# Four heads' base-block products of the recurrence in one run and one PSUM bank, where they stood in two runs and four banks

## The chip, the cores and the metric

The kernel runs on one core of a Trainium2 chip. The metric is the device time of one execution in microseconds (us). The kernel before took 920.47 us, the median of 3 runs (920.27 to 921.49).

## What is computed

Two decoder layers over 512 tokens of width 1024 in fp32. Each layer normalises x, multiplies it with one wide input weight, sends the columns through two branches, multiplies the joined result with an output weight, normalises and adds x. One branch is sliding-window attention; the other, which the change touches, is a gated linear recurrence with 8 heads of a 128x128 state:

```python
def hybrid_layer(x, w_in, w_out, g_pre, g_post, lb, g_head, sinks):
    h = rms_norm(x, g_pre)
    proj = jnp.einsum('bsd,de->bse', h, w_in)
    q_h, f_h, i_h, z_h, q_a, k_a, v_a, z_a = jnp.split(proj, SPLIT_POINTS, axis=-1)
    o_h = hgrn2(q_h, f_h, i_h, lb)
    o_h = rms_norm(o_h, g_head).reshape(B, S, HG_WIDTH).astype(z_h.dtype) * jax.nn.silu(z_h)
    ...
    y = jnp.einsum('bse,ed->bsd', jnp.concatenate([o_h, o_a], axis=-1), w_out)
    return x + rms_norm(y, g_post)

def hgrn2(q, f_logit, i, lb):
    # S_t = diag(f_t) S_{t-1} + (1 - f_t) i_t^T,  o_t = S_t^T q_t
    ...
    def step(state, xs):
        qch, kch, vch, b = xs
        ...
        scores = jnp.einsum('bhtd,bhsd,bhtsd->bhts', qch, kch, decay)
        o = jnp.einsum('bhts,bhsv->bhtv', scores, vch)
        o = o + jnp.einsum('bhtd,bhdv->bhtv', qch * jnp.exp(b), state)
        ...
```

## The kernel before, in words

**Projections.** All weight matrices are split in two fp32r halves (high and low), and each product of a 128-row weight piece takes three matmuls of 128x128 by 128x512 into a PSUM bank of the pool `pj` (3 banks); these are the matmuls of line 293, 3,084 for the two layers' large weights and 192 more for k and v. ScalarE makes the high half of a piece (L181), VectorE or GpSimd the low half (L182). One *step* (`step()`, L276) issues three such matmuls. A table of due times orders the conversions at least 20 steps ahead of the step that needs them.

**The merge.** Everything else runs in between. `merge` (L50) takes several generators, each with a total weight, and always advances the one with the smallest share done; a generator says with each `yield` how much weight it has spent. One of the streams is "the steps up to the end of a slab of weights", 1.0 each. So the weights decide after how many projection steps the next part of the recurrence is issued. In each layer the calls are at L980 to L983: the attention is merged with the steps up to the second slab of f and q columns, `prepare(0)` with the next slab, then `prepare(2)`, `hgrn(0)` and `prepare(4)` in a chain, then `prepare(6)` and `hgrn(4)`. `HG_N` is the total weight that `hgrn` yields. Matmuls issued through `pin` keep their place in the program; other engines' instructions are ordered by a scheduler.

**The recurrence.** The causal 128x128 score matrix of each head and each of four 128-token blocks is built by levels. `prepare(a)` handles heads a and a+1: it makes the scaled copies `qb` and `kb` (L712 to L717) in a pair of temporary tiles, and zeroes the matrix `As` (both heads in one tile of 128x1024, L704). The base products, `spread` (L689), give the 2x2 blocks on the diagonal: 16 matmuls per head, each with a 32-column stationary piece and 32 moving columns, placed on one of four column groups of the array by `tile_position`. In fp32 each is two matmuls in the profile, so a head is 32 matmuls there and two heads are a run of 64. `keep_spread` (L697) copies the valid entries under a mask into `As` with VectorE. Heads a and a+1 with a = 0 or 4 have their spread at the end of `prepare` (L724), into two banks of the pool `sc`; heads a+2 and a+3 have it at the start of `hgrn` (L733), into the two banks of `ac`.

Then `hgrn` does six levels (hh = 2, 4, ... 64). Levels 2 to 16 are a run of 128 matmuls of 32 columns by 16 (L750) for the four heads; level 32 has 64 (L756) and level 64 has 32 (L761). After each level's run, VectorE multiplies q (L768), GpSimd multiplies k (L769), and VectorE (L778) or ScalarE (L783, L788) copies the level's products into `As`. Then come transposes, states and outputs (L796 to L831).

Temporary tiles come from rotating pools: tag `b` has 2 buffers of 128x1024, `s` has 3 of 128x512, `u` has 1 and `a` has 2 of 128x1024.

Of the kernel before, what the change touches and what calls it, by code (L numbers as in the profile page):

```python
# [20 lines left out]
NT = SEQ // 128  # L21
# [11 lines left out]

W_BUFS = 9
RAW_BUFS = 4
HG_N = 53.5
VLAG = 4
QWAIT = 8
ROT_WAIT = 8
# [10 lines left out]
def merge(*streams):  # L50
    live = [[g, 0.0, float(total)] for g, total in streams]
    while live:
        s = min(live, key=lambda e: e[1] / e[2])
        try:
            s[1] += next(s[0]) or 1.0
        except StopIteration:
            live.remove(s)


def chain(*gens):  # L60
    for g in gens:
        yield from g
# [8 lines left out]
def hybrid_kernel(ctx: ExitStack, tc: tile.TileContext, x, wkv, win, wout, g_pre, g_post, lbp, ghead, sinks,  # L71
                  gcol_c, cos_f, sin_f, cos_t, sin_t, masks_c, out):
    nc = tc.nc
    P = 128
# [9 lines left out]
    def pin(ins):  # L84
        return tc.keep_in_program_order(ins)
# [8 lines left out]
    def sc():  # L94
        sc_turn[0] += 1
        return sc_tiles[sc_turn[0] % SC]

    def ac():
        ac_turn[0] += 1
        return ac_tiles[ac_turn[0] % len(ac_tiles)]  # L100

    def tmp(tag, dt=F32, n=1):

        t = tp.tile([P, n, 512] if n > 1 else [P, 512], dt, tag=tag, name=tag, bufs=TB[tag])
        return t
# [25 lines left out]
    for l in range(1, DEPTH):  # L131
        i = plan_order.index((l, "kv"))
# [224 lines left out]
    def halves(tag):  # L357
        t = tmp(tag, n=2)
        return [t[:, 0], t[:, 1]]
# [8 lines left out]
    class Norm:  # L368
# [47 lines left out]
        def rest(self, c):  # L416
            self.turn(c)
            self.high(c)
            self.low(c)
            if self.tt == NT - 1 and c == 1:  # L420
                state["limit"] = None
# [21 lines left out]
    def layer(l, last):  # L443
# [240 lines left out]

        on = {}

        As, kbs, qbs, tots, quad = {}, {}, {}, {}, {}

        def spread(j, bank):  # L689

            for n in range(NT):
                for b in range(4):
                    c = slice(n * P + 32 * b, n * P + 32 * b + 32)
                    pin(nc.tensor.matmul(bank[32 * b:32 * b + 32, c], lhsT=kbs[j][:, c], rhs=qbs[j][:, c], start=True, stop=True,
                                         tile_position=(0, 32 * b)))

        def keep_spread(j, bank):  # L697
            nc.vector.copy_predicated(As[j].rearrange("p (n t) -> p n t", n=NT), bmask.unsqueeze(1).broadcast_to([P, NT, P]),
                                      bank.rearrange("p (n t) -> p n t", n=NT))

        def prepare(a):

            t = tmp("a", n=2)
            nc.gpsimd.memset(t, 0.0)  # L704
            blocks = lambda t, w: t.rearrange("p (b j) -> p b j", j=w)
            for j in range(a, a + 2):
                As[j] = t[:, j - a]
                f, k, q = quad[j] = fT.pop(j), kT.pop(j), qT.pop(j)
                f2, k2, q2 = (blocks(t, 2) for t in (f, k, q))
                qb, kb = halves("b")  # L710
                qb2, kb2 = blocks(qb, 2), blocks(kb, 2)
                nc.vector.reciprocal(kb2[:, :, 1], f2[:, :, 1])  # L712
                nc.scalar.copy(qb2[:, :, 0], q2[:, :, 0])
                nc.vector.tensor_tensor(qb2[:, :, 1], q2[:, :, 1], f2[:, :, 1], op=ALU.mult)
                nc.scalar.copy(kb2[:, :, 0], k2[:, :, 0])
                nc.vector.tensor_tensor(kb2[:, :, 1], kb2[:, :, 1], k2[:, :, 1], op=ALU.mult)
                qbs[j], kbs[j] = qb, kb  # L717

                nc.gpsimd.tensor_tensor(k2[:, :, 0], k2[:, :, 0], f2[:, :, 1], op=ALU.mult)
                nc.vector.tensor_tensor(q2, qb2, f2[:, :, 0].unsqueeze(2).broadcast_to([P, SEQ // 2, 2]), op=ALU.mult)  # L720
                nc.vector.tensor_tensor(f2[:, :, 0], f2[:, :, 0], f2[:, :, 1], op=ALU.mult)
                tots[j] = f2[:, :, 0]
                yield 3.5
            if a % 4 == 0:  # L724
                banks = [sc(), sc()]
                for i in range(2):
                    spread(a + i, banks[i])
                for i in range(2):
                    keep_spread(a + i, banks[i])

        def hgrn(a):
            hs = [(j, *quad.pop(a + j)) for j in range(4)]
            banks = [ac(), ac()]  # L733
            for i in range(2):
                spread(a + 2 + i, banks[i])
            for i in range(2):
                keep_spread(a + 2 + i, banks[i])
            yield 1.5
            for hh in (2, 4, 8, 16, 32, 64):
                nb = SEQ // (2 * hh)  # L740
                per, qu = nb // NT, nb // NT // 4
# [1 line left out]
                for j, f, k, q in hs:  # L743
                    L, i = Ls[j // 2], j % 2
                    qv = q.rearrange("p (b two j) -> p b two j", two=2, j=hh)
                    if hh <= 16:
                        for n in range(NT):
                            for b in range(4):
                                o_, blk, c = n * P + 32 * b, n * per + b * qu, 256 * i + n * 64 + 16 * b
                                pin(nc.tensor.matmul(L[32 * b:32 * b + 32, c:c + 16], lhsT=k[:, o_:o_ + 32],  # L750
                                                     rhs=qv[:, blk:blk + qu, 1, :], start=True, stop=True, tile_position=(0, 32 * b)))
                    elif hh == 32:
                        for n in range(NT):
                            for b in range(2):
                                o_, r_, c = n * P + 64 * b, 64 * b + 32 * (n % 2), 64 * i + n // 2 * 32
                                pin(nc.tensor.matmul(L[r_:r_ + 32, c:c + 32], lhsT=k[:, o_:o_ + 32],  # L756
                                                     rhs=q[:, o_ + 32:o_ + 64], start=True, stop=True, tile_position=(0, r_)))
                    else:
                        for n in range(NT):
                            o_, b, c = n * P, n % 2, 128 * i + n // 2 * 64  # L760
                            pin(nc.tensor.matmul(L[64 * b:64 * b + 64, c:c + 64], lhsT=k[:, o_:o_ + 64],  # L761
                                                 rhs=q[:, o_ + 64:o_ + 128], start=True, stop=True))
                for two in (hs[:2], hs[2:]):
# [9 lines left out]
                    for j, f, k, q in two:  # L773
                        A, L, i = As[a + j], Ls[j // 2], j % 2
# [200 lines left out]
        def run():  # L975
            rest = lambda key: (through(key), remaining(key))
            until(lambda: 1 in qs)
            for _ in range(QWAIT):
                step()
            merge((att_stream([(g, n) for g in range(4) for n in range(NT)]), 4 * NT + VLAG + SLOW[0] * (SLOW[1] - 1)), rest(("in", l, FQ)))  # L980
            merge((prepare(0), 7.0), rest(("in", l, FQ + 1)))
            merge((chain(prepare(2), hgrn(0), prepare(4)), HG_N + 14), rest(("in", l, FQ + 3)))
            merge((chain(prepare(6), hgrn(4)), HG_N + 7), rest(("out", l, "h0")))  # L983
            kv_room.add(l + 1)
            drain(through(("out", l, "h1")))
# [47 lines left out]
    m, n = head[0], head[1]  # L1033
# [43 lines left out]
    amask, bmask = masks[:, 0:128], masks[:, 128:256]  # L1077
# [40 lines left out]
    for run in [layer(l, l == DEPTH - 1) for l in range(DEPTH)]:  # L1118
        run()
# [60 lines left out]
```

## Time and profile before

| | us | share of the span |
|---|---|---|
| profiled execution, its own time | 920.82 | |
| its span, first to last instruction | 919.1 | |
| TensorE matmuls (PE) busy | 903.7 | 98% |
| weight loads (PEld) busy | 751.6 | 82% |
| VectorE (DVE) busy | 668.2 | 73% |
| ScalarE (ACT) busy | 464.2 | 51% |
| GpSimd (POOL) busy | 273.7 | 30% |
| VectorE copies of `keep_spread` (L698), 16 | 10.9 | 1.2% |

The granted TensorE clock was 0.999 of full speed over the span. Rows of the timeline give start and duration of an instruction or of a merged series of equal ones; matmuls overlap their successors, so the distance between two starts says what a matmul costs, not its duration.

### The profile page before, as it was taken

The numbers are of one execution on the slowest core, as the hardware profiler recorded it, in microseconds if no ns is written. First come the engines' busy times: TensorE is split into PE (matmuls) and PEld (weight loads), VectorE is DVE, ScalarE is ACT, GpSimd is POOL, SyncE is SP. The second block draws the span as 40 slices with busy tenths as digits, with TensorE's granted clock in tenths as the row PEclk, the third lists the DMA queues.
The fourth block names the chain that finished last, engine by engine and source line by source line (L and its number), as shares of the span: only waits on it lengthen the run. The fifth ranks groups of instructions, "written<-read, shape, count | busy, mean of one in ns | idle before, by whom it ended". The sixth has DMA issues, their size and how long they took to land.

```text
span 919.1 us, 19004 instructions
## 1 busy us (share of the span) xinstructions
PE 903.7 (98%) x7240; PEld 751.6 (82%) x7240; DVE 668.2 (73%) x1326; ACT 464.2 (51%) x1100; POOL 273.7 (30%) x292
## 2 busy tenths in 40 slices
PE   8999999999999999999999999999999999999997
PEld 6888887888888888888888877888788888888885
DVE  5968877869854896655787689876889439866556
ACT  5535757652755422534464466686446463245242
POOL 3335443303413142121332254450134022330102
PEclk9999999999999999999999999999999999999999
DMA  6584612323222332333356557223322323213413
GB/s 225 184 241 135 166 38 86 92 84 102 71 70 69 121 99 73 92 103 115 116 165 190 161 148 173 58 70 92 94 71 82 93 78 95 82 47 93 138 35 137
DMA packets 56570, 100.74 MB, mean 110 GB/s; under 512 B 6560, under 2 KB 9120, under 8 KB 56480
## 3 DMA queue, kind: packets, MB, share of 16 engines
q1 hardware_dynamic: 56192, 99.40, 36.7%
q8 instruction: 57, 0.93, 0.4%
q14 instruction: 33, 0.27, 0.1%
q10 hardware_dynamic: 288, 0.14, 0.1%
HBM read 86.93 MB, written 12.58 MB: 108 GB/s over the span
## 4 chain that ended last, share of the span: by engine, by line
PE 88%; DVE 6%; ACT 2%; issue 1%; POOL 1%; DMA 0%; POOLq 0%; DVEq 0%; SPq 0%; ACTq 0%
PE pj L293 73%; PE sc L750 2%; PE sc L567 2%; PE ac L620 2%; PE ac L821 2%; DVE wlo L182 1%; PE ac L824 1%; PE ac L808 1%; ACT s L581 1%; PE sc L594 1%; PE sc L873 1%; PE sc L406 1%; PE sc L796 1%; DVE mx L572 0%; DVE a L340 0%
## 5 line engine op out<-in xcount | busy, mean ns | idle before, releaser
L182 DVE TENSOR_TENSOR wlo<-raw,whi 128x512 fp32r<-128x512 f32 x249 | 182.8, 748 | 51.4 <-ACT whi L181 50.6
L181 ACT CAST whi<-raw 128x512 fp32r<-128x512 f32 x256 | 154.2, 620 | 106.0 <-PE pj L293 92.7
L293 PE MATMUL pj<-hhi,wlo 128*128 128x512 f32 x512 | 203.7, 398 | 0.0
L293 PE MATMUL pj<-hhi,whi 128*128 128x512 f32 x512 | 199.7, 390 | 0.0
L293 PE MATMUL pj<-hlo,whi 128*128 128x512 f32 x512 | 199.5, 390 | 0.0
L293 PE MATMUL pj<-whi,ops 128*128 128x512 f32 (+1 forms) x520 | 172.5, 394 | 0.0
L293 PEld LDWEIGHTS pj<-hhi,whi 128*128 128x128 f32 x512 | 96.1, 188 | 20.7
L293 PEld LDWEIGHTS pj<-whi,ops 128*128 128x128 f32 x520 | 97.2, 188 | 19.3
L293 PEld LDWEIGHTS pj<-hhi,wlo 128*128 128x128 f32 x512 | 96.2, 188 | 19.1
L293 PEld LDWEIGHTS pj<-hlo,whi 128*128 128x128 f32 x512 | 96.3, 188 | 18.6
L293 PE MATMUL pj<-whi,hlo 128*128 128x512 f32 x256 | 103.5, 405 | 0.0
L293 PE MATMUL pj<-wlo,ops 128*128 128x512 f32 (+1 forms) x260 | 100.8, 388 | 0.0
L293 PE MATMUL pj<-wlo,hhi 128*128 128x512 f32 x256 | 100.4, 392 | 0.3 <-DVE wlo L182 0.2
L293 PE MATMUL pj<-whi,hhi 128*128 128x512 f32 x256 | 100.3, 392 | 0.0
L769 POOL TENSOR_TENSOR k<-k,tot 128x256 f32<-128x256 f32 x80 | 64.2, 832 | 107.1 <-PE sc L750 57.8
L581 ACT ACTIVATE s<-sc,negm 128x128 f32<-128x128 f32 x128 | 45.6, 368 | 38.7 <-DVE negm L575 38.7
L768 DVE TENSOR_TENSOR q<-q,tot 128x256 f32<-128x256 f32 x80 | 48.8, 648 | 12.7 <-PE sc L756 6.9
L293 PEld LDWEIGHTS pj<-whi,hhi 128*128 128x128 f32 x256 | 48.1, 188 | 10.2
L293 PEld LDWEIGHTS pj<-wlo,ops 128*128 128x128 f32 x260 | 49.0, 188 | 8.8
L293 PEld LDWEIGHTS pj<-wlo,hhi 128*128 128x128 f32 x256 | 48.3, 189 | 8.9 <-DVE wlo L182 1.0
L293 PEld LDWEIGHTS pj<-whi,hlo 128*128 128x128 f32 x256 | 48.2, 188 | 8.0
L588 POOL TENSOR_TENSOR s<-s,sums 128x512 f32<-128x512 f32 x32 | 34.1, 1067 | 44.3 <-DVE sums L586 28.6
(188 smaller groups left out, 1417.0 us busy)
## 6 DMA issues: line engine op xcount, KB each, us to landing
raw<-in_win_dram SPq DMA_DIRECT2D x192, 256.0 KB, 2.7
raw<-in_wout_dram SPq DMA_DIRECT2D x64, 256.0 KB, 2.7
stack<-rot SPq DMA_DIRECT2D x16, 512.0 KB, 3.4
qs<-stack SPq DMA_DIRECT2D x32, 256.0 KB, 4.7
a<-in_x_dram SPq DMA_DIRECT2D x12, 256.0 KB, 3.5
raw<-in_wkv_dram SPq DMA_DIRECT2D x8, 256.0 KB, 3.9
x_mid<-a SPq DMA_DIRECT2D x8, 256.0 KB, 2.8
a<-x_mid SPq DMA_DIRECT2D x8, 256.0 KB, 3.2
```

Of the source, the lines that this page charges most:

```text
L181: keep(nc.scalar.copy(hi, v))
L182: keep((nc.gpsimd if i in on_pool and i % 2 else nc.vector).tensor_tensor(lo, v, hi.bitcast(F32), op=ALU.subtract))
L293: nc.tensor.matmul(u.o, lhsT=u.sta(k, u.w)[i], rhs=u.mov(k, u.w)[j], start=(n == 0), stop=(n == len(u.list) - 1))
L406: pin(nc.tensor.transpose(o[:, j * P:(j + 1) * P], self.xn[:, c, j * P:(j + 1) * P], ident))
L567: pin(nc.tensor.matmul(S[:, h * 256:(h + 1) * 256], lhsT=q[:, 2 * hp_ + h, t_], rhs=kst[v][p][:, (n - 1) * P:(n + 1) * P], start=(h == 0 a ...
L581: nc.scalar.activation(pt[:, h * P:(h + 1) * P], cur[h], AF.Exp, bias=negm[:, h:h + 1], scale=SCALE, accum_out=sums[:, h:h + 1])
L588: nc.gpsimd.tensor_tensor(pv, pv, sums.unsqueeze(2).broadcast_to([P, 4, P]), op=ALU.mult)
L620: pin(nc.tensor.matmul(U, lhsT=vst[v][:, blk, :], rhs=d, start=(i == 0), stop=(i == len(terms) - 1)))
L750: pin(nc.tensor.matmul(L[32 * b:32 * b + 32, c:c + 16], lhsT=k[:, o_:o_ + 32], rhs=qv[:, blk:blk + qu, 1, :], start=True, stop=True, tile_ ...
L768: nc.vector.tensor_tensor(qv[:, :, 1, :], qv[:, :, 1, :], tv[:, :, 0].unsqueeze(2).broadcast_to([P, nb, hh]), op=ALU.mult)
L769: nc.gpsimd.tensor_tensor(kv_[:, :, 0, :], kv_[:, :, 0, :], tv[:, :, 1].unsqueeze(2).broadcast_to([P, nb, hh]), op=ALU.mult)
L821: pin(nc.tensor.matmul(O[:, c], lhsT=A[:, c], rhs=vs(j, n), start=(n == 0), stop=False))
```

## The change

All four heads' base products now form one run at the start of `hgrn`, into one bank of `ac`. The bank holds only the 32 columns that each product gives (before, each product was written at its own place in a full 128x512 bank). `keep_spread` copies two heads at once: two masked copies of 128x1024 for four heads, where there were four of 128x512, reading the 32 columns four times by a broadcast. `prepare` no longer issues matmuls. The copies `qb` and `kb` of heads a+2 and a+3 take tiles of the tags `s` and `u`, since those of heads a and a+1 now stay in tag `b` until the run. The first `yield` of `hgrn` is 3.0 in place of 1.5, and `HG_N` is 55.0 in place of 53.5.

```diff
-HG_N = 53.5
+HG_N = 55.0
...
-        def spread(j, bank):
-
-            for n in range(NT):
-                for b in range(4):
-                    c = slice(n * P + 32 * b, n * P + 32 * b + 32)
-                    pin(nc.tensor.matmul(bank[32 * b:32 * b + 32, c], lhsT=kbs[j][:, c], rhs=qbs[j][:, c], start=True, stop=True,
-                                         tile_position=(0, 32 * b)))
+        def spread(a, bank):
+
+            for j in range(4):
+                for n in range(NT):
+                    for b in range(4):
+                        c, o_ = slice(n * P + 32 * b, n * P + 32 * b + 32), P * j + 32 * n
+                        pin(nc.tensor.matmul(bank[32 * b:32 * b + 32, o_:o_ + 32], lhsT=kbs[a + j][:, c], rhs=qbs[a + j][:, c],
+                                             start=True, stop=True, tile_position=(0, 32 * b)))
...
-            nc.vector.copy_predicated(As[j].rearrange("p (n t) -> p n t", n=NT), bmask.unsqueeze(1).broadcast_to([P, NT, P]),
-                                      bank.rearrange("p (n t) -> p n t", n=NT))
+            for i in range(2):
+                nc.vector.copy_predicated(pairs[a + 2 * i].rearrange("p j (n b t) -> p (j n) b t", n=NT, b=4),
+                                          bmask.rearrange("p (b t) -> p b t", b=4).unsqueeze(1).broadcast_to([P, 2 * NT, 4, 32]),
+                                          bank[:, 256 * i:256 * i + 256].rearrange("p (m t) -> p m t", t=32).unsqueeze(2)
+                                          .broadcast_to([P, 2 * NT, 4, 32]))
...
-                qb, kb = halves("b")
+                qb, kb = halves("b") if a % 4 == 0 else (tmp("s"), tmp("s" if j == a else "u"))
...
-            if a % 4 == 0:
-                banks = [sc(), sc()]
-                for i in range(2):
-                    spread(a + i, banks[i])
-                for i in range(2):
-                    keep_spread(a + i, banks[i])
...
-            banks = [ac(), ac()]
-            for i in range(2):
-                spread(a + 2 + i, banks[i])
-            for i in range(2):
-                keep_spread(a + 2 + i, banks[i])
-            yield 1.5
+            bank = ac()
+            spread(a, bank)
+            keep_spread(a, bank)
+            yield 3.0
```

What TensorE has in its program before, around the base products of the first layer's heads 0 to 3: `pj` are projections, `sc` and `ac` the PSUM banks of the recurrence, and x16 counts matmuls of the program (two each in the profile). The first dots leave out 47 projection matmuls, the second 6.

```order
L293 MATMUL pj<-hhi,whi 128x512
L694 MATMUL sc_79<-b 32x32 x16
L694 MATMUL sc_80<-b 32x32 x16
L293 MATMUL pj<-hhi,wlo 128x512
...
L694 MATMUL ac_82<-b 32x32 x16
L694 MATMUL ac_81<-b 32x32 x16
L293 MATMUL pj<-hhi,wlo 128x512
L293 MATMUL pj<-hlo,whi 128x512
L293 MATMUL pj<-hhi,whi 128x512
...
L750 MATMUL sc_78<-q,k 32x16 x32
L750 MATMUL sc_79<-q,k 32x16 x32
```

The same place in the changed kernel; the dots leave out 15 projection matmuls.

```order
L293 MATMUL pj<-hhi,whi 128x512
L695 MATMUL ac_82<-b 32x32 x32
L695 MATMUL ac_82<-s 32x32 x16
L695 MATMUL ac_82<-s,u 32x32 x16
L293 MATMUL pj<-hhi,wlo 128x512
L293 MATMUL pj<-hlo,whi 128x512
L293 MATMUL pj<-hhi,whi 128x512
...
L747 MATMUL sc_79<-q,k 32x16 x32
L747 MATMUL sc_80<-q,k 32x16 x32
```

The first run of 64 is gone from its place, the second is now a run of 128, and 18 projection matmuls stand between it and the first level's run where there were 9. The other three groups of four heads moved in the same way.

On VectorE, the preparation of head 2 before, behind the copies of the first run (the tile `b` is the one that the first run read):

```order
L182 TENSOR_TENSOR wlo<-raw,whi 128x512 x6
L698 COPY_PREDICATED a<-masks,sc_79 128x512
L698 COPY_PREDICATED a<-masks,sc_80 128x512
L712 RECIPROCAL b<-f 128x256
L714 TENSOR_TENSOR b<-q,f 128x256
L716 TENSOR_TENSOR b<-b,k 128x256
```

In the changed kernel the two reciprocals of heads 2 and 3 stand ahead, and one series of copies comes later, behind the run of 128:

```order
L717 RECIPROCAL s<-f 128x256
L182 TENSOR_TENSOR wlo<-raw,whi 128x512 x2
L721 TENSOR_TENSOR s<-s,k 128x256
L717 RECIPROCAL u<-f 128x256
...
L851 TENSOR_TENSOR ops<-z_2286,ops 128x512
L700 COPY_PREDICATED a<-masks,ac_82 128x1024 x2
```

The preparation of heads 2 and 3 no longer stands behind the copies of heads 0 and 1.

More of the change, by code (lines that the diff above doesn't have):

```diff
@@ L685, in layer, with keep_spread @@
         on = {}
-        As, kbs, qbs, tots, quad = {}, {}, {}, {}, {}
-        def spread(j, bank):
-            for n in range(NT):
-                for b in range(4):
-                    c = slice(n * P + 32 * b, n * P + 32 * b + 32)
-                    pin(nc.tensor.matmul(bank[32 * b:32 * b + 32, c], lhsT=kbs[j][:, c], rhs=qbs[j][:, c], start=True, stop=True,
-                                         tile_position=(0, 32 * b)))
-        def keep_spread(j, bank):
-            nc.vector.copy_predicated(As[j].rearrange("p (n t) -> p n t", n=NT), bmask.unsqueeze(1).broadcast_to([P, NT, P]),
-                                      bank.rearrange("p (n t) -> p n t", n=NT))
+        As, pairs, kbs, qbs, tots, quad = {}, {}, {}, {}, {}, {}
+        def spread(a, bank):
[5 more added lines that the diff above has]
+                                             start=True, stop=True, tile_position=(0, 32 * b)))
+        def keep_spread(a, bank):
+            for i in range(2):
[3 more added lines that the diff above has]
+                                          .broadcast_to([P, 2 * NT, 4, 32]))
         def prepare(a):
@@ L704, in prepare @@
             nc.gpsimd.memset(t, 0.0)
+            pairs[a] = t
             blocks = lambda t, w: t.rearrange("p (b j) -> p b j", j=w)
```

## The prediction

> **What bounds the kernel now.** I read the page first: its busy times, and the chain that ended last.
>
> ```profile
> span 919.1 us, 19004 instructions
> PE 903.7 (98%) x7240; PEld 751.6 (82%) x7240; DVE 668.2 (73%) x1326; ACT 464.2 (51%) x1100; POOL 273.7 (30%) x292
> PE 88%; DVE 6%; ACT 2%; issue 1%; POOL 1%; DMA 0%; POOLq 0%; DVEq 0%; SPq 0%; ACTq 0%
> ```
>
> TensorE is busy 98% of the span and carries 88% of the last chain. So a change counts by what it takes from TensorE's own row of work, or by a wait that it puts there. The profiled execution took 920.82 us, 1.72 over its span and 0.35 over the median of 920.47; I make the sum against 920.82 and take 0.35 off at the end.
>
> Second, the timeline of TensorE around one run of base products. A projection matmul starts every 0.227 us: (195.78 - 189.66) / 27, since 27 starts lie between these two rows.
>
> ```profile
> 189.66 0.39 PE L293 MATMUL pj<-hhi,whi 128*128 128x512 f32 x1
> ...
> 195.78 0.39 PE L293 MATMUL pj<-hhi,whi 128*128 128x512 f32 x1
> 196.10 0.76 PE L694 MATMUL sc<-b 128*32 128x32 f32 x64
> 196.79 0.51 PE L293 MATMUL pj<-hhi,wlo 128*128 128x512 f32 x1
> 197.13 0.39 PE L293 MATMUL pj<-hlo,whi 128*128 128x512 f32 x1
> ```
>
> The run is entered 0.32 us after the last projection (not 0.227), and the first projection behind it takes 0.34. From 195.78 to 197.13 are 1.35 us, which hold two projection matmuls (0.45): the run of 64 costs 0.90 us.
>
> Third, how a run of 128 looks. The first level's runs have the same form, with 16 columns for 32; here is a short one, and the longest that shows no gap named by the profile.
>
> ```profile
> 349.86 0.39 PE L293 MATMUL pj<-whi,ops 128*128 128x512 f32 x1
> 350.18 1.32 PE L750 MATMUL sc<-q,k 128*32 128x16 f32 x128
> 351.43 0.50 PE L293 MATMUL pj<-whi,ops 128*128 128x512 f32 x1
> 351.77 0.40 PE L293 MATMUL pj<-wlo,ops 128*128 128x512 f32 x1
> ```
>
> ```profile
> 238.28 0.39 PE L293 MATMUL pj<-hhi,whi 128*128 128x512 f32 x1
> 238.60 1.42 PE L750 MATMUL sc<-q,k 128*32 128x16 f32 x128
> 239.95 0.50 PE L293 MATMUL pj<-hhi,wlo 128*128 128x512 f32 x1
> 240.29 0.39 PE L293 MATMUL pj<-hlo,whi 128*128 128x512 f32 x1
> ```
>
> By the same count they cost 1.91 - 0.45 = 1.46 us and 2.01 - 0.45 = 1.56. Twice as many matmuls as a run of 64 cost 0.56 to 0.66 more, not 0.90: about 0.3 of each run is the change from full-width matmuls to column groups and back.
>
> Fourth, two of the sixteen such runs are longer, both directly behind a run of base products: in the second half of layer 1 and in the first half of layer 2.
>
> ```profile
> 319.87 0.39 PE L293 MATMUL pj<-hhi,whi 128*128 128x512 f32 x1
> 320.19 1.66 PE L750 MATMUL sc<-q,k 128*32 128x16 f32 x128
> 321.78 0.50 PE L293 MATMUL pj<-hhi,wlo 128*128 128x512 f32 x1
> 322.11 0.39 PE L293 MATMUL pj<-hlo,whi 128*128 128x512 f32 x1
> ```
>
> ```profile
> 660.54 0.76 PE L694 MATMUL ac<-b 128*32 128x32 f32 x64
> 661.23 0.51 PE L293 MATMUL pj<-hhi,wlo 128*128 128x512 f32 x1
> ...
> 663.16 0.39 PE L293 MATMUL pj<-hhi,whi 128*128 128x512 f32 x1
> 663.48 1.23 PE L750 MATMUL sc<-q,k 128*32 128x16 f32 x115
> 664.92 0.31 PE L750 MATMUL sc<-q,k 128*32 128x16 f32 x13 [0.21 <-issue]
> 665.15 0.50 PE L293 MATMUL pj<-hhi,wlo 128*128 128x512 f32 x1
> 665.49 0.40 PE L293 MATMUL pj<-hlo,whi 128*128 128x512 f32 x1
> ```
>
> They cost 2.24 - 0.45 = 1.79 and 2.33 - 0.45 = 1.88 us. The second broke off after 115 matmuls, within one head's work, and the profile names no engine for it, only "issue". That is no wait for data; it looks like TensorE's own instructions not being there. The page's queue of instructions:
>
> ```profile
> q8 instruction: 57, 0.93, 0.4%
> ```
>
> 57 packets of 16.3 KB serve TensorE's 7,240 matmuls and 7,240 loads, about 254 instructions or 127 pairs each. Back from the break, 115 pairs, 9 projections and 3 pairs of the run before are one packet: run through in some 3.5 us (from 661.2 to 664.7).
>
> **The change part by part.**
>
> *Switching.* Each of the four groups (two layers, two halves) has one run where it had two. It saves 2 x 0.90 - 1.46 = 0.34 us at best and 2 x 0.90 - 1.56 = 0.24 at worst. Nothing else counts on TensorE here: the 512 base matmuls stay 512, at about 9 ns each. I take 0.32, near the short run, since the new run waits for other engines only at two of its heads. 4 x 0.32 = 1.28 us (0.96 to 1.36), all of it on the path.
>
> *The break in the first level's run.* 18 projections in place of 9 now stand between the run and the level's. A packet that spans both runs must hold all 18, so it takes at least 18 x 0.227 = 4.08 us and 0.3 for the switching, over the 3.5 (plus 0.2 of waiting) that was too short. I therefore expect both breaks to go: 1.79 + 1.88 - 2 x 1.48 = 0.71 us, with 1.48 for an ordinary run. The ends are 0 (the break comes all the same) and 0.71; I take 0.70.
>
> The Trainium skill (Runtime: NRT & Kernel Launch, section Instruction fetch mechanics) says that instructions come in blocks of 16 KiB, 256 at a time, fetched while the current block runs, and that crossing a block's edge is mostly hidden. The trace agrees with the size and, for fourteen of the sixteen runs, with the hiding; by the rule taken strictly the two breaks would have another cause and could stay.
>
> *The copies on VectorE.*
>
> ```profile
> L698 DVE COPY_PREDICATED a<-masks,sc 128x512 f32<-128x512 uint8 x8 | 5.5, 747 | 5.7 <-PE sc L694 5.7
> L698 DVE COPY_PREDICATED a<-masks,ac 128x512 f32<-128x512 uint8 x8 | 5.4, 730 | 0.0
> L778 DVE COPY_PREDICATED a<-masks,sc 128x256 f32<-128x256 uint8 x64 | 28.8, 510 | 0.0
> ```
>
> 16 copies of 0.74 (10.9 us) become 8 of 128x1024. By the step from 256 to 512 columns (0.23 us) one takes 0.74 + 2 x 0.23 = 1.2; by two of the old ones, 1.5. So 9.6 to 12 us: nothing gained or lost. Queued behind the block of 2.4 to 3.0 us on VectorE are low halves of weights and the first level's q. TensorE's waits for low halves are 0.2 us in the whole run:
>
> ```profile
> L293 PE MATMUL pj<-wlo,hhi 128*128 128x512 f32 x256 | 100.4, 392 | 0.3 <-DVE wlo L182 0.2
> ```
>
> A conversion is made 20 steps ahead, 20 x 3 x 0.227 = 13.6 us, which covers 3.0. The first level's q is not touched before its own run, 4.1 us later. If neither cover held, 3 us a group would show.
>
> *The wait for the fourth head.* The run of 128 needs all four heads' copies. In both halves the last input in the trace is ready well before the second run of today:
>
> ```profile
> 203.71 0.42 DVE L716 TENSOR_TENSOR b<-b,k 128x256 f32<-128x256 f32 x1
> ```
>
> ```profile
> 207.88 0.76 PE L694 MATMUL ac<-b 128*32 128x32 f32 x64
> ```
>
> ```profile
> 311.65 0.42 DVE L716 TENSOR_TENSOR b<-b,k 128x256 f32<-128x256 f32 x1
> ```
>
> ```profile
> 317.25 0.76 PE L694 MATMUL ac<-b 128*32 128x32 f32 x64
> ```
>
> 3.7 and 5.2 us of slack. The run of 128 keeps that place, 47 or more projections behind, and VectorE's order puts the reciprocals earlier since they no longer wait for tile `b`. I cost it at nothing. Tiles `s` and `u` are free there: their users, attention and the outputs of the half before, are done. No DMA moves, and SP's order is the same; GpSimd has the same instructions.
>
> *Shift of the levels.* `HG_N` grows by what the first `yield` grows, so the end of `hgrn` moves by under one step in the merge. The first gap between levels falls from 33 projections to 30 in the first half, 6.8 us. GpSimd's four products for a level take 4 x 0.83 = 3.3 us and still fit.
>
> ```profile
> L769 POOL TENSOR_TENSOR k<-k,tot 128x256 f32<-128x256 f32 x80 | 64.2, 832 | 107.1 <-PE sc L750 57.8
> ```
>
> Sum: 920.82 - 1.28 - 0.70 = 918.84 for a profiled execution, 918.5 as a median.
>
> **The rivals.** A measurement of this kernel can tell about 0.2% (1.84 us) from no change; the line is at 918.63, so my forecast lies just beyond it.
>
> (a) The breaks have another cause and stay (the strict rule above): only 1.28 is saved, 920.47 - 1.28 = 919.2. For it: the level's run breaks off in only two of four groups. Against it: no wait for an engine is named.
>
> (b) The change moves the shortage and does not remove it: two runs of 128 lie 4.1 us apart, 256 pairs where there were 192, and break in all four groups by 0.33 to 0.40. 4 x 0.37 = 1.5 in place of 0.7: 920.47 - 1.28 + 0.8 = 920.0.
>
> (c) Slower. TensorE takes its matmuls in order; if head 3's or 7's copies come late, everything behind the run of 128 waits. Each us of lateness costs 4. It becomes a loss over 0.2% beyond (1.98 + 1.84) / 4 = 0.95 us late; at 1.0 the time is 918.5 + 4.0 = 922.5. Against it stand the slacks of 3.7 and 5.2 us.
>
> (d) Faster still. The largest wait of TensorE's loads for an engine is in the attention:
>
> ```profile
> PEld sc L567 <- ACT s L581: 7.5, 16, 1.2
> ```
>
> Layer 2's attention runs behind the changed part, and with its start moved one such wait may go: 918.5 - 1.2 = 917.3. It may as well come.
>
> **How the numbers follow.** Forecast 0.60, (a) 0.15, (b) 0.10, (c) 0.05, (d) 0.10. The forecast has ends of 0.96 to 1.36 for the switching and some 0.5 either way for waits elsewhere, 918.0 to 919.3; with its centre 0.13 under the line I give it 0.37 faster and 0.23 same. With (d), faster is 0.47; with (a) and (b), same is 0.48; slower is (c), 0.05. The range takes in (d) and (b) with half a us above it: 917.3 to 920.5. Likeliest is 918.5.
>
> **What would show it.** In the profile after: four runs of 128 base matmuls (L695) of 1.3 to 1.4 us in the timeline, entered in 0.32; four first-level runs (L747) of 1.32 to 1.42 with no "issue" gap; eight copies (L700) of 1.2 to 1.5 us; no idle time of PE or PEld before L695 that names DVE or ACT. A span more than 1 us off 917.1 with these in place would mean that waits elsewhere moved; a first-level run of 1.6 or more would be (a) or (b), an idle time before L695 (c).

## The result, and the profile after

| | median, us | lowest to highest | executions |
|---|---|---|---|
| before, same chip | 921.07 | 920.27 to 921.79 | 10 |
| changed kernel | 918.77 | 918.37 to 919.24 | 10 |

The ratio is 0.9977, 95% interval 0.9968 to 0.9985: 1.4 to 2.9 us faster, which leaves out no change and straddles the prediction's 0.2% line (1.84 us). A second measurement of the same kernel, on another chip (below), gave 0.9977 again, 0.9967 to 0.9986. The profiled execution took 918.41 us, where the prediction's sum said 918.84. The medians set against each other say 2.3 us, where 1.98 were forecast.

The page of the changed kernel, to be set beside the first fence of the prediction:

```profile
span 916.7 us, 18998 instructions
PE 902.5 (98%) x7240; PEld 751.6 (82%) x7240; DVE 673.0 (73%) x1318; ACT 462.9 (50%) x1100; POOL 268.5 (29%) x292
PE 89%; DVE 6%; ACT 2%; issue 1%; POOL 1%; DMA 0%; POOLq 0%; DVEq 0%; SPq 0%; ACTq 0%
```

The bound is where it was, on TensorE, with the same 7,240 matmuls. The difference must be in how they follow each other. TensorE's timeline (start, duration, operation, count) around a run of 128 base products, in the second layer's first half. The view splits the run where the names of its operands change (the dots leave out rows of single matmuls); it is one run:

```profile
657.77 0.39 PE L293 MATMUL pj<-hhi,whi 128*128 128x512 f32 x1
658.09 0.73 PE L695 MATMUL ac<-b 128*32 128x32 f32 x62
...
658.67 0.45 PE L695 MATMUL ac<-s 128*32 128x32 f32 x30
658.97 0.46 PE L695 MATMUL ac<-s,u 128*32 128x32 f32 x32
659.36 0.50 PE L293 MATMUL pj<-hhi,wlo 128*128 128x512 f32 x1
659.69 0.40 PE L293 MATMUL pj<-hlo,whi 128*128 128x512 f32 x1
```

From 657.77 to 659.69 are 1.92 us; less two projections (0.45), the run costs 1.47. The slowest of the four is the first one:

```profile
206.12 0.39 PE L293 MATMUL pj<-hhi,whi 128*128 128x512 f32 x1
206.44 0.73 PE L695 MATMUL ac<-b 128*32 128x32 f32 x62
...
207.02 0.45 PE L695 MATMUL ac<-s 128*32 128x32 f32 x30
207.45 0.46 PE L695 MATMUL ac<-s,u 128*32 128x32 f32 x32
207.84 0.50 PE L293 MATMUL pj<-hhi,wlo 128*128 128x512 f32 x1
208.18 0.40 PE L293 MATMUL pj<-hlo,whi 128*128 128x512 f32 x1
```

1.61 us here: the fourth head's matmuls (operands `s,u`) begin 0.43 us behind the third's row here and 0.30 in the fence above. And the two first-level runs that broke off before:

```profile
320.76 0.39 PE L293 MATMUL pj<-hhi,whi 128*128 128x512 f32 x1
321.07 1.34 PE L747 MATMUL sc<-q,k 128*32 128x16 f32 x128
322.34 0.50 PE L293 MATMUL pj<-hhi,wlo 128*128 128x512 f32 x1
322.68 0.39 PE L293 MATMUL pj<-hlo,whi 128*128 128x512 f32 x1
```

```profile
663.36 0.39 PE L293 MATMUL pj<-hhi,whi 128*128 128x512 f32 x1
663.68 1.35 PE L747 MATMUL sc<-q,k 128*32 128x16 f32 x128
664.96 0.50 PE L293 MATMUL pj<-hhi,wlo 128*128 128x512 f32 x1
665.29 0.39 PE L293 MATMUL pj<-hlo,whi 128*128 128x512 f32 x1
```

Both are whole, with no row that says "issue", and cost 1.47 and 1.48 us (1.92 and 1.93, less 0.45), where they cost 1.79 and 1.88.

The same count, made for every such run of every kernel in this study, gives the table that the rest of the text goes by. "Base" is the sum of all runs of base products, "first level" the sum of the four first-level runs behind them, in the order of the program. Each cost is good to about 0.01 us, as the rows are rounded, so the sums are good to some 0.05.

| kernel | span, us | base, us | first level, us each | sum of both | median, us | ratio to before |
|---|---|---|---|---|---|---|
| before | 919.1 | 7.20 (8 runs) | 1.52 1.79 1.88 1.47 | 13.86 | | |
| changed | 916.7 | 6.05 (4) | 1.47 1.47 1.47 1.47 | 11.92 | 918.77 | 0.9977 |
| e1_gap_only | 918.7 | 7.19 (8) | 1.47 1.47 1.47 1.49 | 13.08 | 920.41 | 0.9992 |
| e2_merge_near | 919.9 | 5.93 (4) | 2.13 1.94 1.47 1.67 | 13.14 | 921.27 | 1.0002 |
| e3_merge_adjacent | 929.6 | with the first level | 4.99 6.77 4.81 5.24 | 21.80 | 931.29 | 1.0114 |
| e4_four_runs | 922.4 | 9.47 (16) | 1.48 1.47 1.47 1.47 | 15.35 | 924.75 | 1.0038 |
| e5_shift_blocks | 920.6 | 7.20 (8) | 1.57 1.47 1.47 2.00 | 13.71 | 921.92 | 1.0013 |
| e6_two_banks | 917.9 | 5.92 (4) | 1.47 1.47 1.47 1.47 | 11.78 | 919.43 | 0.9983 |
| e7_halves_one_bank | 917.9 | 7.17 (8) | 1.47 1.47 1.47 1.47 | 13.04 | 919.91 | 0.9990 |
| e8_more_between | 917.6 | 5.96 (4) | 1.47 1.47 1.47 1.47 | 11.82 | 919.07 | 0.9981 |
| e9_changed_again | 917.2 | 6.09 (4) | 1.47 1.47 1.47 1.47 | 11.96 | 919.60 | 0.9977 |
| e10_two_banks_again | 918.0 | 6.02 (4) | 1.47 1.47 1.49 1.47 | 11.91 | 919.71 | 0.9977 |

Of the 2.4 us between the two spans, 13.86 - 11.92 = 1.94 lie in these runs. Some 0.5 more lie far ahead of the change, at some 12 us of the span, in TensorE's wait for GpSimd's part of the first weights (tile `wkv`): 1.2 us before, 0.6 in the changed kernel. In the other profiles this wait was 0.6 (e2, e3, e4, e7, e8, e9) or 1.1 (e1, e5, e6, e10). The two kernels that were profiled twice showed the same value both times (0.6 for the changed one, 1.1 for the one with two banks), so it may belong to the program and not to the execution; that was not tried. Either way it is no part of what the change was made for.

### The profile page after: what moved, and what is told of

Same layout as the page of the kernel before. It is cut to its first block, busy times and chain, and to the rows that moved or that the text cites. A ratio compares the mean times of both kernels' runs of the same rounds, so it can differ in the third digit from the quotient of the medians.

```text
span 916.7 us, 18998 instructions
## 1 busy us (share of the span) xinstructions
PE 902.5 (98%) x7240; PEld 751.6 (82%) x7240; DVE 673.0 (73%) x1318; ACT 462.9 (50%) x1100; POOL 268.5 (29%) x292
## 4 chain that ended last, share of the span: by engine, by line
PE 89%; DVE 6%; ACT 2%; issue 1%; POOL 1%; DMA 0%; POOLq 0%; DVEq 0%; SPq 0%; ACTq 0%
PE pj L293 73%; PE sc L747 2%; PE sc L567 2%; PE ac L620 2%; PE ac L818 2%; DVE wlo L182 1%; PE ac L821 1%; PE ac L805 1%; PE sc L594 1%; ACT s L581 1%; PE sc L870 1%; PE sc L406 1%; PE ac L695 1%; PE sc L793 1%; DVE mx L572 1%
## 5 line engine op out<-in xcount | busy, mean ns | idle before, releaser
L766 POOL TENSOR_TENSOR k<-k,tot 128x256 f32<-128x256 f32 x80 | 60.9, 789 | 113.4 <-PE sc L747 65.9
L765 DVE TENSOR_TENSOR q<-q,tot 128x256 f32<-128x256 f32 x80 | 52.8, 701 | 14.4 <-PE sc L747 8.4
```

The source lines that it names most:

```text
L765: nc.vector.tensor_tensor(qv[:, :, 1, :], qv[:, :, 1, :], tv[:, :, 0].unsqueeze(2).broadcast_to([P, nb, hh]), op=ALU.mult)
L766: nc.gpsimd.tensor_tensor(kv_[:, :, 0, :], kv_[:, :, 0, :], tv[:, :, 1].unsqueeze(2).broadcast_to([P, nb, hh]), op=ALU.mult)
```

## The experiments

The theory has two parts. One: each run of column-group matmuls costs about 0.3 us for going over to them and back, whatever its length, so that four runs for eight save 1.2. Two: the breaks come when two dense runs lie so close that TensorE uses up a packet of instructions before the next has come; 18 projections between the runs prevent that. The rivals are that the breaks belong to their place in the program, and that the gain comes from the one bank, or from the new order on VectorE. Before's medians on the experiments' chips were 921.18 (e1 to e4), 920.85 (e5 to e8) and 921.40 us (e9, e10).

**The distance alone.** The kernel before, with its runs of 64 as they are and twice the projections ahead of the first level:

```diff
-HG_N = 53.5
+HG_N = 55.0
 ...
-            yield 1.5
+            yield 3.0
```

> The kernel before with only its spacing changed: the two runs of 64 per group stay, and 18 projection matmuls in place of 9 stand between the second and the first level's run. Theory (switching 0.3 us a run, and TensorE short of its own instructions when a run and a half come within 4 us): the switching is not touched, the two breaks of 0.33 and 0.40 us in the first level's runs go, all four first-level runs last 1.32 to 1.42 us; 0.6 us faster than before (0.3 to 0.9). Rival A (the breaks have another cause): two first-level runs still last 1.6 us or more, no difference from before. Rival B (the whole gain comes from the preparation no longer waiting for tile b on VectorE): no difference either, and the breaks as they were.

Measured: 920.41 us, ratio 0.9992 (0.9983 to 1.0001), 0.77 under the kernel before. All four first-level runs are ordinary (1.47 to 1.49 us); one that had broken, from this kernel's timeline:

```profile
322.01 0.39 PE L293 MATMUL pj<-hhi,whi 128*128 128x512 f32 x1
322.33 1.34 PE L750 MATMUL sc<-q,k 128*32 128x16 f32 x128
323.59 0.50 PE L293 MATMUL pj<-hhi,wlo 128*128 128x512 f32 x1
323.93 0.39 PE L293 MATMUL pj<-hlo,whi 128*128 128x512 f32 x1
```

1.92 - 0.45 = 1.47. The base runs cost what they did, 7.19, so the sum falls by 0.78, nearly all of it in the breaks. The interval of the time reaches to no change; that the breaks go with the distance alone rests on the runs' costs, and falls in with the time.

**One run, without the distance.** The changed kernel with the old numbers:

```diff
-HG_N = 55.0
+HG_N = 53.5
 ...
-            yield 3.0
+            yield 1.5
```

> The changed kernel with 9 projection matmuls behind the run of 128 instead of 18. Theory: the switching of four runs is saved (1.2 us), but a block of 256 instructions can now begin in the run of 128 and end in the level's run after only 9 projections, and by the places of the blocks this happens in all four groups: four first-level runs of 1.6 to 1.75 us, 4 x 0.35 = 1.4 lost against 0.7 before; 0.6 us faster than before (0.2 to 0.9), 1.3 slower than the changed kernel. Rival A: no breaks that depend on the spacing, so as fast as the changed kernel or with the two old breaks, 1.2 to 2.0 us faster than before. Rival B: as fast as the changed kernel, 2 us faster than before.

Measured: 921.27 us, ratio 1.0002 (0.9993 to 1.0011). The runs do as the theory says: base 5.93, and breaks in three of the four groups. The longest:

```profile
210.40 0.40 PE L293 MATMUL pj<-hhi,whi 128*128 128x512 f32 x1
210.72 0.72 PE L747 MATMUL sc<-q,k 128*32 128x16 f32 x63
211.97 0.75 PE L747 MATMUL sc<-q,k 128*32 128x16 f32 x65 [0.52 <-issue]
212.64 0.50 PE L293 MATMUL pj<-hhi,wlo 128*128 128x512 f32 x1
212.98 0.39 PE L293 MATMUL pj<-hlo,whi 128*128 128x512 f32 x1
```

2.58 - 0.45 = 2.13. But the expected time, 0.6 under the kernel before, was missed: the runs' sum is 0.7 below and the span 0.8 above. Part of the rest has names in the waits. The output projection now waits for its gated operand, which it doesn't in the changed kernel:

```profile
PEld pj L293 <- DVE ops L851: 1.1, 2, 0.7
```

and the attention's wait for ScalarE, the one of the prediction's rival (d), is 3.5 us in sum on TensorE where it was 2.9. So the merge alone won 1.27 us on the base runs and left nothing: 0.55 went to the breaks (7.21 - 6.66), and the rest to waits that moved, which are read from one profile and were not tried further.

**Both runs back to back.** The changed kernel without the `yield`, so that 128 base products and the first level's 128 form one stretch of 256:

```diff
-HG_N = 55.0
+HG_N = 52.0
 ...
-            yield 3.0
```

> The changed kernel with no projection between the run of 128 and the first level's run, so 256 small matmuls follow each other. Theory: two more switches per group are saved (four groups, 1.0 us more than in the changed kernel), but a whole block of 256 instructions and more runs through in 1.4 us where its successor takes 3.9 us to come: a break of about 2.5 us in each group, 10 us in all; 7 us slower than before (4 to 9). Rival A: the switching alone counts, 2.3 to 3.0 us faster than before. Rival B: 2 to 3 us faster.

Measured: 931.29 us, ratio 1.0114 (1.0099 to 1.0129), 10.1 slower and beyond what was expected. All four groups break, by 2.4, 3.7, 2.2 and 2.6 us. The longest break, and the clock behind it (window, its length, busy time and count for each engine, granted clock, DMA share, GB/s):

```profile
318.77 1.30 PE L746 MATMUL sc<-q,k 128*32 128x16 f32 x117
323.58 0.39 PE L746 MATMUL sc<-q,k 128*32 128x16 f32 x10 [3.51 <-issue]
323.90 0.80 PE L293 MATMUL pj<-hhi,wlo 128*128 128x512 f32 x1
324.49 0.63 PE L293 MATMUL pj<-hlo,whi 128*128 128x512 f32 x1
...
326.20 0.63 PE L293 MATMUL pj<-hhi,whi 128*128 128x512 f32 x1
326.63 0.50 PE L293 MATMUL pj<-hhi,wlo 128*128 128x512 f32 x1
```

```profile
323.50:326.50 3.00, 2.92 (x16) 2.41 (x17) 0.40 (x2) 0.92 (x2) 0.84 (x1) 0.50 0.04 14
```

The runs cost 21.80 - 13.86 = 7.9 us more than in the kernel before, which is the size that was expected. What came on top is the clock of TensorE that the profile shows as granted: it is 0.50 behind this break, and projections start every 0.43 us, (326.63 - 324.49) / 5, not 0.227. That is 5 x 0.2 = 1.0 us here and some 1.5 at 671.5 us; 7.9 + 2.5 = 10.4, and the spans differ by 10.5. The mechanism of the breaks was right, the lost clock was not thought of.

**More switches.** The run of 128 cut into four of 32 with 9 projections between (one head each, `spread` called per head):

```diff
+            for j in range(4):
+                spread(a, bank, [j])
+                if j < 3:
+                    yield 1.5
             keep_spread(a, bank)
```

> The changed kernel with its run of 128 cut into four runs of 32, one for each head, 6 or 9 projections between them, one bank and two copies as in the changed kernel. Theory: 12 more runs than in the changed kernel at 0.31 us each, 3.7 us slower than it and 1.9 us slower than before (1.4 to 2.4); no breaks. Rival A: the same switching, and two breaks stay: 2.5 us slower than before. Rival B: the switching is nothing, and VectorE's order is as in the changed kernel: 2 us faster than before.

Measured: 924.75 us, ratio 1.0038 (1.0025 to 1.0051). One run of 32:

```profile
205.65 0.39 PE L293 MATMUL pj<-hhi,whi 128*128 128x512 f32 x1
205.97 0.46 PE L695 MATMUL ac<-b 128*32 128x32 f32 x32
206.35 0.50 PE L293 MATMUL pj<-hhi,wlo 128*128 128x512 f32 x1
206.69 0.39 PE L293 MATMUL pj<-hlo,whi 128*128 128x512 f32 x1
```

1.04 - 0.45 = 0.59 us. With 0.90 for 64 and 1.47 for 128 the three sizes lie on a line: 0.30 + 32 x 0.009, 0.30 + 64 x 0.0093, 0.30 + 128 x 0.0091. So a run's price is 0.3 us and some 9.1 ns for each matmul; 12 runs more cost 9.47 - 6.05 = 3.42 us, 0.285 each. Against the kernel before that makes 2.3 more for the base runs and 0.8 less for the breaks, 1.5 in sum; measured were 3.6, more than the 1.4 to 2.4 that were expected. What the other 2 us are is only in part known: the out-projection waits for its gated operand again (two conversions of it, on VectorE and on ScalarE).

```profile
PEld pj L293 <- DVE ops L854: 1.6, 2, 0.8
PEld pj L293 <- ACT ops L853: 0.9, 2, 0.4
```

**The same kernel with its instructions shifted.** Nothing of the order around the breaks is touched; only the number of instructions ahead of it changes:

```diff
+    for i in range(40):
+        c = 32 * (i % 4)
+        pin(nc.tensor.matmul(warm[c:c + 32, 0:32], lhsT=ones[:, 0:32], rhs=ones[:, 0:32], start=True, stop=True, tile_position=(0, c)))
```

> The kernel before, with 40 throwaway column-group matmuls of 32 columns put behind the warm-up matmul at the start; nothing else is touched. They only move where the edges of TensorE's instruction packets fall in everything that follows. Theory (breaks come where a packet of instructions is used up before the next is there): the two breaks of 0.3 to 0.4 us change their groups; the first-level runs at about 320 and 663 us become ordinary (cost 1.45 to 1.55 us), and one or both of those at about 211 and 773 us get a break (cost 1.8 to 1.9 us). Rival (a cause fixed to the place in the program, such as a late operand): the breaks stay at 320 and 663 us. Time by both: within 1.5 us of the kernel before, since the added matmuls take at most about 1 us at the start, ahead of the first weights.

Measured: 921.92 us, ratio 1.0013 (1.0004 to 1.0022), within the 1.5 us; the runs cost 0.15 us less in sum, so what it is longer lies outside them. The 40 are 80 matmuls in the profile, with 80 loads. The breaks moved to the two groups named, in full in one and in small in the other (1.57 us at 211). The group at 773 us, which had no break, and the one at 320, which had one:

```profile
773.66 0.39 PE L293 MATMUL pj<-hhi,whi 128*128 128x512 f32 x1
773.98 0.91 PE L750 MATMUL sc<-q,k 128*32 128x16 f32 x82
775.23 0.61 PE L750 MATMUL sc<-q,k 128*32 128x16 f32 x46 [0.35 <-issue]
775.78 0.50 PE L293 MATMUL pj<-hhi,wlo 128*128 128x512 f32 x1
776.11 0.39 PE L293 MATMUL pj<-hlo,whi 128*128 128x512 f32 x1
```

```profile
320.45 0.39 PE L293 MATMUL pj<-hhi,whi 128*128 128x512 f32 x1
320.77 1.33 PE L750 MATMUL sc<-q,k 128*32 128x16 f32 x128
322.04 0.50 PE L293 MATMUL pj<-hhi,wlo 128*128 128x512 f32 x1
322.37 0.39 PE L293 MATMUL pj<-hlo,whi 128*128 128x512 f32 x1
```

2.45 - 0.45 = 2.00 and 1.92 - 0.45 = 1.47. A cause that belongs to the place (a late operand, an engine, a transfer of data) would have stayed at 320 and 663 us.

What they follow can be read from the traces in two ways. The first is a count of the matmuls that have started up to a time. Here it is for the moment when TensorE stands still in the second group, in the kernel before and in e3_merge_adjacent (window, length, PE busy and count, granted clock, DMA share, GB/s):

```profile
0.00:321.40 321.40, 316.56 (x2484) 1.00 0.41 120
```

```profile
0.00:323.50 323.50, 313.91 (x2484) 1.00 0.42 121
```

Both stop after the same matmul, and so does e2_merge_near, though the projections between the runs differ. The second is the instruction queue of the prediction (q8), whose single packets the trace dates to a tenth of a microsecond. In the kernel before, one is moved at 318.7, and it is the only one between 318.7 and 320.1:

```profile
q8 instruction: 1, 0.02, 5.5%
```

| stop | matmuls started by then | time that the last 126 of them took, us | TensorE goes on at | after the packet was moved, by us |
|---|---|---|---|---|
| before, 2nd and 3rd group | 2,484 and 4,880 | 3.4 to 3.5 | 321.49 and 664.93 | 2.8 and 2.5 |
| e2_merge_near, 1st, 2nd, 4th | 1,220, 2,484, 6,018 | 3.4 to 3.5 | 211.97, 321.86, 773.58 | 2.6, 2.4, 2.8 |
| e3_merge_adjacent, all four | 1,220, 2,484, 4,881, 6,018 | 1.2 | 211.49, 323.59, 670.46, 781.88 | 2.2, 2.5, 2.5, 2.8 |
| e5_shift_blocks, 4th | 6,145 | 3.4 | 775.24 | 3.0 |

From group to group the counts lie 1,264, 2,396 or 2,397, and 1,137 apart, which is 10, 19 and 9 times 126 to 127 matmuls; each has its weight load, so this is some 253 instructions, the prediction's 254 of a packet. The 6,145 of e5_shift_blocks is 127 behind the 6,018 of the others: its 80 matmuls more at the start carry the packets' edges to other places of the program, and the count still fits. At every stop a packet was moved 2.2 to 3.0 us before TensorE went on; in the longest break (e3, second group) it was moved 1.2 us after TensorE had stopped. So TensorE stops at a packet's edge because the next packet is not there; counted from the edge before, it could go on after 3.3 to 4.9 us.

The same counts lie inside the first-level runs of the changed kernel and of e1_gap_only too (in the second group these are the matmuls 2,385 to 2,512). There the last 126 matmuls take 5.3 us or more, as they hold at least 18 projections, and TensorE runs over the edge without a stop; the next packet had been moved 3.2 us before or earlier. So the distance did not move the edges out of the runs, it gave the packet its time. What stays open is why one packet comes sooner than another: in e2_merge_near the edge at 4,880 was passed without a stop after 3.5 us, with the packet moved 2.7 us before, while the other three groups broke off.

**One bank or two.** The changed kernel with heads 0 and 1 of a group in one bank and heads 2 and 3 in another:

```diff
-            bank = ac()
-            spread(a, bank)
-            keep_spread(a, bank)
+            banks = [ac(), ac()]
+            spread(a, banks)
+            keep_spread(a, banks)
```

> The changed kernel with its run of 128 written into two accumulator banks (64 matmuls in each) in place of one; order, copies and projections as in the changed kernel. Theory (the gain comes from fewer switches and from the distance of the two runs): the one bank brings nothing, 918.9 us, that is 2.0 to 2.4 us under the kernel before, each run of 128 at 1.45 to 1.6 us. Rival (the one bank itself saves time): above 919.8.

Measured: 919.43 us, ratio 0.9983 (0.9974 to 0.9992): 1.4 under the kernel before by the medians, between the two expectations, though the runs cost no more than in the changed kernel (11.78 us and 11.92). To compare them without a change of chip, both ran side by side:

> The changed kernel as it is, once more, on one chip with the next one, so that the two can be compared directly. 2.0 to 2.4 us under the kernel before; the four runs of 128 at 6.0 us in sum and the four first-level runs at 5.9.

> The changed kernel with the run of 128 in two banks, on the same chip as the changed kernel. Theory (the bank is of no account; the 0.5 us by which two banks fell short was a difference between chips and executions): within 0.4 us of the changed kernel. Rival (one bank saves time by itself): 0.5 us or more above it.

Measured: 919.60 us with one bank, ratio 0.9977 (0.9967 to 0.9986), and 919.71 with two, ratio 0.9977 (0.9968 to 0.9987). By the medians both are 1.7 and 1.8 under the kernel before, a little less than the 2.0 to 2.4 expected. They differ by 0.1: the bank is of no account for the time. Of the profiled executions the one with two banks is 0.8 us longer (spans 917.2 and 918.0). In it, as in e6_two_banks, the wait for `wkv` (1.1 for 0.6) and the attention's wait for ScalarE (3.6 and 3.4 for 2.7) are longer; the medians show no such difference.

**Old runs, new tiles and copies.** The changed kernel's tiles, its one bank and its two big copies, but the run cut in two halves at the old places:

```diff
+            if a % 4 == 0:
+                early[a] = ac()
+                spread(a, early[a], (0, 1))
 ...
-            bank = ac()
-            spread(a, bank)
+            bank = early.pop(a)
+            spread(a, bank, (2, 3))
             keep_spread(a, bank)
```

> The changed kernel's tiles, masked copies and one bank, but the run of 128 cut into two runs of 64 at the places where the kernel before has them; 18 projections stay between the second and the first level's run. Theory: the switching of eight runs comes back (8 x 0.90 us against 6.05), the breaks stay away: 1.2 us slower than the changed kernel, 0.8 to 1.2 us under the kernel before. Rival (the two big copies on VectorE and their places bring the gain): 2.0 us or more under the kernel before.

Measured: 919.91 us, ratio 0.9990 (0.9981 to 0.9999), 0.94 under the kernel before, inside the 0.8 to 1.2 of the theory. The base runs cost 7.17 again, and nothing breaks. This kernel has the new tiles and copies, e1_gap_only the old ones, and both have the distance: 0.94 here and 0.77 there, each with an interval of some 0.8 either way, so a gain from VectorE's order is not seen, and one of a few tenths is not ruled out.

**More distance.** The changed kernel with half as many projections again:

```diff
-HG_N = 55.0
+HG_N = 56.5
 ...
-            yield 3.0
+            yield 4.5
```

> The changed kernel with the first level's run half as far again behind the run of 128 (pause of 4.5 in place of 3.0, about 27 projections between). Theory (two dense runs need only to be some 4 us apart, which 18 projections give): nothing more to win, within 0.4 us of the changed kernel's 918.8, unless the out-projection has to wait for its gated operand, which a later first level can hold back on VectorE: then 0.3 to 1.0 us above it. Rival (each projection between still buys time): 0.4 us or more under the changed kernel.

Measured: 919.07 us, ratio 0.9981 (0.9972 to 0.9989). The runs cost 11.82 us in sum, as in the changed kernel: 18 projections are enough, and 27 give nothing more that can be told.

## Why the prediction was right

Its forecast was the case that came: both savings, and no new wait in the changed part. That the median hit 918.5 to 0.3 us is in part luck: the kernel before took 921.07 on this chip, 0.6 above the 920.47 that the sum started from, and the gain was 0.3 larger than forecast. By its steps:

*Switching, 1.28 us (0.96 to 1.36).* Measured 7.20 - 6.05 = 1.15, inside its ends. The three sizes of run put the price of one switch at 0.285 to 0.30 us, so the reading of "about 0.3 of each run" from the runs of 64 and of 128 was right. I took 0.32, the better end, because the run "waits for other engines only at two of its heads"; three of the four runs had that (1.47 to 1.50), the first cost 1.61.

*The breaks, 0.70 us.* Measured 6.66 - 5.87 = 0.79 over the four groups: 0.32 and 0.41 for the two. The other 0.06 is a small delay in the first one, which the prediction had passed over; it is no break, since it comes after 96 matmuls, where the fourth head begins, and not at the count of 1,220. The cause that the prediction gave holds: with the distance alone they go (e1_gap_only), without it they come back (e2_merge_near), with no distance they grow to 2.2 us and more (e3_merge_adjacent), and they move when only instructions are counted on (e5_shift_blocks). The prediction's border was loose, though on the safe side: it set 4.08 + 0.3 us, for projections and switching alone, against 3.5 us that had the small matmuls in them as well. With its 108 small ones such a packet lasts 5.4 us. That is longer than the 4.9 us after which TensorE could go on at the latest (e3_merge_adjacent); 4.4 us would not have been. The rule of the Trainium skill (Runtime: NRT & Kernel Launch, section Instruction fetch mechanics), that a block's edge is mostly hidden, holds for runs with 18 projections between them; at 9 ns a matmul it doesn't hold for closer ones, and the strict reading, rival (a), falls.

*The copies, nothing.* The copies took 1.32 us each, between the 1.2 and the 1.5 of the estimate, 10.5 us in sum where 10.9 went before:

```profile
L700 DVE COPY_PREDICATED a<-masks,ac 128x1024 f32<-128x1024 uint8 x8 | 10.1, 1318 | 9.3 <-PE ac L695 9.3
```

VectorE sits idle for 9.3 us ahead of them, where it was 5.7, so what stands behind them in its order can come later; TensorE's wait for low halves is 0.2 us as before. VectorE's busy time rose by 4.8 us all the same. Its products of q take 7.6 us more (16 of 588 ns before, of 832 after, and 80 of 648 and of 701), other rows less. They are as long in e1_gap_only (835 and 702 ns), so this goes with the distance and not with the copies or the tiles; nothing on TensorE waits longer for it.

*The wait for the fourth head, nothing.* No idle time before L695 names VectorE or ScalarE. Rival (c) had its slack, and more: the last inputs of the fourth head are written more than 7 us ahead of the run at 206.44, since the reciprocals no longer wait for tile `b`. On VectorE the last one is this row, on ScalarE a copy that starts at 198.71 and takes 0.43:

```profile
198.34 0.42 DVE L719 TENSOR_TENSOR s<-q,f 128x256 f32<-128x256 f32 x1 [1.19 <-ACT q L680]
```

The 0.13 us inside the first run, at the fourth head, is therefore no late operand. What it is stays open; a semaphore of TensorE's own queue stands at that place, and the delay was there in two of the five other profiles that have this run on its own (e9_changed_again and e10_two_banks_again, not e2_merge_near, e6_two_banks and e8_more_between).

*Rivals (b) and (d).* (b), a shortage in all four groups, did not come, but its idea was sound: with 9 projections between the runs, e2_merge_near is that case in three of four groups. (d) didn't come: the attention's wait stands at 2.6 us in sum on TensorE, and stood at 2.9.

The chances of "faster" and "same" were about even because the forecast lay at the 0.2% line, and so does the result. The profiled execution came 0.43 under the sum, which is about the 0.5 of the wait at 12 us and no credit of the working.

## What to carry to other kernels

Count the cost of a stretch of small column-group matmuls from the start of the last full one ahead to the start of the second behind it, for two or three sizes: the part that doesn't grow with the size (0.3 us here) is what joining two stretches saves. Then look how much dense work lies within a few microseconds of it: a break that the profile puts down to "issue" and that moves when instructions are added far ahead is a shortage of instructions. The instruction queue's packets in the profile confirm it: here one was moved 2.2 to 3.0 us before the engine went on. Count how long a packet's worth of instructions takes across both stretches (3.5 us was mostly too short here, 5.4 enough); full-width matmuls put between (18 here, 4.1 us) cure it, while joining without them gives the gain back. When the order shifts, read the waits of the whole span, since one that appears far from the change can be as large as the gain.

## What the runs showed that was not expected

A break of TensorE can cost twice. In e3_merge_adjacent the granted clock fell to one half behind two of the four breaks, the one of 3.7 us and the shortest, 2.2 us (at 670 us; there the half clock came 1.2 us after the break's end and lasted 3.4 us), and not behind those of 2.4 and 2.6 us. The Trainium skill (TensorE: Matmul & The Clock Gate, Part 1) puts the fall to half clock after an idle window of about 3.4 us; the first of the two agrees, the second doesn't fit that number, and the breaks of under 1 us never did it here.

The gated operand of the output projection has next to no slack in the second half of each layer: in e2_merge_near and e4_four_runs, where the first level stands elsewhere against it, TensorE's loads waited 1.1 us and 2.5 us for it (0.5 in e3_merge_adjacent), and in the kernels before and after not at all.
